# Smaller first and last chains on VectorE, a slightly changed preference on TensorE, and the last store on another queue, in an attention kernel

## Chip, cores, metric

One core of one Trainium2 chip. The metric is device time in microseconds (us); several executions of each kernel are timed, and kernels that are compared ran on the same chip in the same rounds. A few executions fell into a slow state (lower granted TensorE clock, 415 us and more); they are left out of the times and ratios below. All ratios compare with the kernel before in the same rounds.

## The reference

Grouped-query attention: 8 batches, 8 query heads, 2 key/value heads, 1024 positions, head size 64, float32.

```python
scores = scale * np.matmul(q_group, k_group.transpose(0, 1, 3, 2))
scores_max = np.max(scores, axis=-1, keepdims=True)
attn = np.exp(scores - scores_max)
attn = attn / (np.sum(attn, axis=-1, keepdims=True) + 1e-08)
output[:, q_start:q_end, :, :] = np.matmul(attn, v_group)
```

## The kernel before

The work is cut into 128 jobs (batch, head, half of the queries) of 8 cells (128 keys by 512 queries); a cell's exponentials are 65,536 numbers. ScalarE takes most cells, two at a time, with its exponential. VectorE takes some, with a bit trick: one instruction turns scores into the bits of a power of two (`p1`, L491), and then a **chain** of four steps corrects a group of cells at once: "and" (VectorE), "line" (GpSimd), "prod" and "add" (VectorE, two SBUF inputs each). TensorE computes the scores ("qk"), and, when a cell's exponentials are ready, the output ("pv"); VectorE normalises a finished job.

The order of all instructions is fixed beforehand by a planner, a small model inside the kernel. Each engine then works its list strictly in order, so one late step holds back everything behind it.

```python
GROUP, PARTS = 10, 2
CHAIN = ("and", "line", "prod", "add")
ON_POOL = ("line",)

def make_plan(nj, nkc):
    ...
    LIVE_A, LIVE_D, PENDING, PER_JOB, LEAD, RAMP, AHEAD, FIRST_PV = 28, 5, 16, 2, 6, 6, 0.0, 2.0
    AHEAD_D, EXTRA, LAST = 0, 0, 6
    ...
        if job_a < nj:                      # a score cell for ScalarE
            ...
                best = min(best or (INF,), (t - AHEAD, 1, "qk", 0, t))
        if job_d < nj and job_d <= job_a + lead + 1 and pending < PENDING:   # one for VectorE
            ...
        for i, (at, _, _, step) in enumerate(chainq):
            if CHAIN[step] in ON_POOL:
                at = max(at, pool, two_end)     # a line waits for VectorE's step to end
            else:
                at = max(at, dve, pool)         # and VectorE's step for the line
    ...
        elif kind == "p1":
            ...
            cur.append(cell)
            if len(cur) == GROUP:
                chainq.append((dve, d_id, cur, 0))
                cur = []
# ... (cut)
    def put_out(b, h, sides):
        rows = "(s p two) d -> p s two d"
        nc.sync.dma_start(
            out=out[b, h].rearrange(rows, p=128, two=2)[:, :, sides],
            in_=stage[(b, h)][:, :, sides],
        )
# ... (cut)
            if op[2] >= len(jobs) - 2:                       # the last two jobs: half stores
                at(op[0] + 0.01, put_out, b, h, slice(side, side + 1))
            elif ended.setdefault(op[2] // 2, op[2]) != op[2]:
                at(op[0] + 1.5, put_out, b, h, slice(0, 2))  # else one store for a pair
```

The softmax here doesn't subtract the row's maximum and nothing guards it: scores larger than these inputs give would overflow.

## Time and profile before

| | kernel before |
|---|---|
| time, median of 3 | 385.65 us (385.5 to 385.9) |
| span in the profile | 384.0 us |
| first activation starts / last one ends | 7.40 / 379.43 us |
| activations | 404 of two cells |
| cells on VectorE | 216 of 1024 |

The lines are in the prediction below. ScalarE runs one activation after another for 372 us; the time is their count, times their rhythm, plus what stands before the first and after the last.

### The profile page before, as it was taken

What the parts mean: (1) busy time and instruction counts of PE and PEld (TensorE: products, weight loads), DVE (VectorE), ACT (ScalarE), POOL (GpSimd) and SP (SyncE); (2) the same over time, 40 slices, a digit from 0 to 9 for tenths busy, and PEclk for the clock granted to TensorE, in tenths of its full rate; (3) what the DMA queues carried; (4) which work ended last, traced back from release to release, by engine and by line L of the source; (5) the groups of instructions that cost most, each with busy time, mean ns of one, the idle gap of its engine ahead of it and who ended that gap; (6) DMA issues with size and microseconds to landing.
All of it is one profiled execution on the core that took longest, in us unless ns stands there. A gap on an engine that the chain in (4) does not pass through costs nothing.

```text
span 384.0 us, 12026 instructions
## 1 busy us (share of the span) xinstructions
PE 365.6 (95%) x5172; PEld 233.6 (61%) x5172; DVE 353.8 (92%) x548; ACT 374.6 (98%) x409; POOL 174.4 (45%) x147
## 2 busy tenths in 40 slices
PE   8879898999999999999999999999999999998995
PEld 7425464666666666666666666666666666564664
DVE  4779998999999999999999999999999999989982
ACT  5999999999999999999999999999999999999995
POOL 5584535718244371563718245271643627040420
PEclk9999999999999999999999999999999999999999
DMA  8988988697756848585676759468675765711213
GB/s 137 135 152 135 130 154 124 129 147 140 113 109 132 140 103 139 101 156 103 139 131 120 130 106 152 96 126 137 105 124 123 138 102 119 126 56 29 57 56 84
DMA packets 102485, 45.48 MB, mean 118 GB/s; under 512 B 63792, under 2 KB 100976, under 8 KB 101184
## 3 DMA queue, kind: packets, MB, share of 16 engines
q1 hardware_dynamic: 82096, 31.21, 36.1%
q0 software_dynamic: 19712, 13.18, 32.3%
q8 instruction: 40, 0.66, 0.7%
q10 hardware_dynamic: 624, 0.33, 0.3%
q14 instruction: 13, 0.11, 0.1%
HBM read 25.17 MB, written 27.00 MB: 136 GB/s over the span
## 4 chain that ended last, share of the span: by engine, by line
ACT 86%; PE 10%; DVE 2%; issue 1%
ACT p_ring L477 86%; PE aps L466 4%; PE ops L538 4%; PE ops L409 1%; PE dps L466 1%; DVE pd L527 1%; DVE ost L554 0%; DVE y L525 0%; DVE z L512 0%; DVE rec L551 0%; PE dps L382 0%; PE dps L428 0%; PE ops L428 0%; PE aps L382 0%; DVE blank L288 0%
## 5 line engine op out<-in xcount | busy, mean ns | idle before, releaser
L477 ACT ACTIVATE p_ring<-aps 128x1024 bf16<-128x1024 f32 x404 | 371.8, 1067 | 1.4 <-PE aps L466 1.2
L466 PE MATMUL aps<-qT,kset 128*128 128x512 bf16 x808 | 239.9, 378 | 13.0 <-ACT p_ring L477 12.4
L538 PEld LDWEIGHTS <-p_ring 128*128 128x128 bf16 x3232 | 140.1, 98 | 64.0
L538 PE MATMUL ops<-vset,p_ring 128*128 128x65 bf16 x3232 | 154.6, 194 | 0.0
L491 DVE TENSOR_SCALAR pd<-dps 128x512 uint16<-128x512 f32 x216 | 138.6, 683 | 7.0 <-PE dps L466 6.7
L516 POOL TENSOR_SCALAR y<-z 128x5120 f16<-128x5120 uint16 (+1 forms) x22 | 96.4, 4383 | 70.0 <-DVE rec L551 48.7
L466 PEld LDWEIGHTS <-kset 128*128 128x128 bf16 x1024 | 79.7, 97 | 56.4 <-issue 25.8
L323 POOL DMA_DIRECT2D scr_q<-in_q_dram x63 | 39.1, 621 | 83.5 <-PE dps L466 44.3
L466 PE MATMUL dps<-qT,kset 128*128 128x512 bf16 x216 | 76.4, 379 | 0.0
L525 DVE TENSOR_TENSOR y<-z,y 128x5120 f16<-128x5120 uint16 (+1 forms) x22 | 61.0, 2772 | 1.1 <-POOL y L516 1.1
L527 DVE TENSOR_TENSOR pd<-pd,y 128x5120 uint16<-128x5120 uint16 (+1 forms) x22 | 60.9, 2769 | 0.1
L554 DVE TENSOR_TENSOR ost<-ops,rec 128x256 f32<-128x256 f32 x128 | 54.3, 425 | 4.4
L538 PEld LDWEIGHTS <-pd 128*128 128x128 bf16 x864 | 42.8, 98 | 24.7 <-DVE ost L554 2.2
L538 PE MATMUL ops<-vset,pd 128*128 128x65 bf16 x864 | 52.2, 194 | 0.3
L512 DVE TENSOR_SCALAR z<-pd 128x5120 uint16<-128x5120 uint16 (+1 forms) x22 | 32.3, 1467 | 0.5
L551 DVE RECIPROCAL rec<-ops 128x4 f32<-128x4 f32 x128 | 22.6, 176 | 9.6 <-PE ops L538 8.2
L323 POOL DMA_DIRECT2D scr_k<-in_k_dram x15 | 9.8, 656 | 39.9 <-PE aps L466 33.0
L356 POOL DMA_DIRECT2D vset<-in_v_dram x32 | 24.9, 784 | 0.0
L409 PE MATMUL ops<-blank 128*128 128x128 bf16 x40 | 5.3, 313 | 1.1 <-DVE blank L288 1.1
L409 PEld LDWEIGHTS <-blank 128*128 128x128 bf16 x40 | 4.4, 149 | 1.1 <-DVE blank L288 1.1
L363 POOL DMA_DIRECT2D kset<-kset x6 | 4.1, 684 | 0.0
L420 ACT ACT_TABLE_LOAD x1 | 1.3, 1283 | 1.8 <-issue 1.8
(23 smaller groups left out, 10.2 us busy)
## 6 DMA issues: line engine op xcount, KB each, us to landing
out_dram<-ost SPq DMA_DIRECT2D x63, 256.0 KB, 2.9
scr_q<-in_q_dram POOLq DMA_DIRECT2D x63, 128.0 KB, 3.5
kset<-kT SPq DMA_DIRECT2D x60, 64.0 KB, 3.1
vset<-in_v_dram POOLq DMA_DIRECT2D x32, 64.0 KB, 3.9
scr_k<-in_k_dram POOLq DMA_DIRECT2D x15, 128.0 KB, 3.7
qT<-scr_q SPq DMA_TRANSPOSE x63, 3.5
kset<-kset POOLq DMA_DIRECT2D x6, 128.0 KB, 4.3
fq<-in_q_dram ACTq DMA_DIRECT2D x2, 128.0 KB, 3.3
```

The costliest lines, as they stand in the source:

```text
L323: dma = nc.gpsimd.dma_start(out=scr.rearrange("(p f) -> p f", f=1024), in_=src.rearrange("(p s) d -> p (s d)", s=1024 // D),)
L356: nc.gpsimd.dma_start(out=vsets[b % 2][:, g, two * NHC : (two + 1) * NHC, 0:D], in_=v[b, g].rearrange("(c p two) d -> two p c d", p=128, t ...
L466: last_score[0] = nc.tensor.matmul(dst, lhsT=ksets[b % 2][:, h // HPG, side, c * 128 : (c + 1) * 128], rhs=qT[(b, h)], start=True, stop=Tr ...
L477: act = nc.scalar.activation(out=pt[:, 0:m], in_=psum.pop(("A", n))[:, 0:m], func=AF.Exp, scale=scale)
L491: nc.vector.tensor_scalar(out=groups[g][:, slot], in0=psum.pop(cell), scalar1=bits_scale, scalar2=bits_bias, op0=ALU.mult, op1=ALU.add,)
L512: eng.tensor_scalar(out=z, in0=pd, scalar1=0x7F, scalar2=None, op0=ALU.bitwise_and)
L516: eng.tensor_scalar(out=y, in0=z, scalar1=CURVE_A / 128.0, scalar2=CURVE_B, op0=ALU.mult, op1=ALU.add,)
L525: eng.tensor_tensor(out=y, in0=z, in1=y, op=ALU.mult)
L527: eng.tensor_tensor(out=pd, in0=pd, in1=y, op=ALU.add)
L538: nc.tensor.matmul(ops_of[s][:, qs, :], lhsT=p_of[cell][:, qs * 128 : (qs + 1) * 128], rhs=vsets[b % 2][:, h // HPG, c, :], start=opens an ...
L551: nc.vector.reciprocal(out=rec, in_=o[:, :, D])
L554: nc.vector.tensor_tensor(out=stage[(b, h)][:, :, side, :], in0=o[:, :, 0:D], in1=rec.unsqueeze(2).to_broadcast([128, NQS, D]), op=ALU.mult,)
```

## The change

The intent: let VectorE start on small chains so that its first results come early, end on small ones so that its last results are not late, and save the last store a place behind others on SyncE's queue. The diff, cut to its core (`per_job` with its zeros changes nothing):

```diff
-    ... AHEAD, FIRST_PV = 28, 5, 16, 2, 6, 6, 0.0, 2.0
+    ... AHEAD, FIRST_PV = 28, 5, 16, 2, 6, 6, 0.02, 2.0
+    FIRST_SIZES, FIRST_JOBS, FIRST_MORE = (3, 4, 6, 8), 0, 0
+    LAST_SIZE, LAST_GROUPS, LAST_JOBS, LAST_MORE = 4, 6, 6, 0
+    def size(g):
+        if g < len(FIRST_SIZES):
+            return FIRST_SIZES[g]
+        return LAST_SIZE if job_d >= nj - LAST_GROUPS else GROUP
-            if len(cur) == GROUP:
+            if len(cur) >= size(d_id):
-    def put_out(b, h, sides):
+    def put_out(b, h, sides, queue):
-        nc.sync.dma_start(
+        queue.dma_start(
-                at(op[0] + 0.01, put_out, b, h, slice(side, side + 1))
+                queue = nc.scalar if op[2] == len(jobs) - 1 else nc.sync
+                at(op[0] + 0.01, put_out, b, h, slice(side, side + 1), queue)
```

More of the change, by code (lines that the diff above doesn't have):

```diff
@@ L38, in make_plan @@
     FROM_PE, FROM_PV, FROM_ACT, FROM_DVE, FROM_POOL = 0.21, 0.16, 0.165, 0.10, 0.15
-    LIVE_A, LIVE_D, PENDING, PER_JOB, LEAD, RAMP, AHEAD, FIRST_PV = 28, 5, 16, 2, 6, 6, 0.0, 2.0
+    LIVE_A, LIVE_D, PENDING, PER_JOB, LEAD, RAMP, AHEAD, FIRST_PV = 28, 5, 16, 2, 6, 6, 0.02, 2.0
     INF = 1e9
-    AHEAD_D, EXTRA, LAST = 0, 0, 6
+    AHEAD_D = 0
+    FIRST_SIZES, FIRST_JOBS, FIRST_MORE = (3, 4, 6, 8), 0, 0
+    LAST_SIZE, LAST_GROUPS, LAST_JOBS, LAST_MORE = 4, 6, 6, 0
     FIRST_TURN, FIRST_LOAD, EACH_LOAD = 2.4, 4.5, 4.2
@@ L64, in first_free, with per_job @@
         return min(range(len(slots)), key=lambda s: slots[s])
+    def per_job(j):
+        if j < FIRST_JOBS:
+            return PER_JOB + FIRST_MORE
+        return PER_JOB + LAST_MORE * (j >= nj - LAST_JOBS)
+    def size(g):
+        if g < len(FIRST_SIZES):
+            return FIRST_SIZES[g]
+        return LAST_SIZE if job_d >= nj - LAST_GROUPS else GROUP
     while normed < nj:
@@ L73, in make_plan @@
         while job_d < nj and (
-            taken[job_d] >= PER_JOB + EXTRA * (job_d >= nj - LAST)
+            taken[job_d] >= per_job(job_d)
             or not todo[job_d]
@@ L576 @@
             if op[2] >= len(jobs) - 2:
-                at(op[0] + 0.01, put_out, b, h, slice(side, side + 1))
+                queue = nc.scalar if op[2] == len(jobs) - 1 else nc.sync
+                at(op[0] + 0.01, put_out, b, h, slice(side, side + 1), queue)
             elif ended.setdefault(op[2] // 2, op[2]) != op[2]:
-                at(op[0] + 1.5, put_out, b, h, slice(0, 2))
+                at(op[0] + 1.5, put_out, b, h, slice(0, 2), nc.sync)
         at(op[0], run[op[1]], *op[2:])
```

## The prediction

> **What bounds the kernel now.** I read the page's busy shares and its chain first, then the groups by line, then three short stretches of the timeline (start of the chain, about 30 us, about 368 us) and the end.
>
> ```profile
> PE 365.6 (95%) x5172; PEld 233.6 (61%) x5172; DVE 353.8 (92%) x548; ACT 374.6 (98%) x409; POOL 174.4 (45%) x147
> ...
> ACT 86%; PE 10%; DVE 2%; issue 1%
> ...
> L477 ACT ACTIVATE p_ring<-aps 128x1024 bf16<-128x1024 f32 x404 | 371.8, 1067 | 1.4 <-PE aps L466 1.2
> L466 PE MATMUL aps<-qT,kset 128*128 128x512 bf16 x808 | 239.9, 378 | 13.0 <-ACT p_ring L477 12.4
> ```
>
> ScalarE's exponentials (L477) are 371.8 of the 384.0 us span and had 1.4 us of visible idle, 1.2 of it before the first one. It is a single string: first start 7.40 us, last start 378.35 us, 403 spacings, so 370.95 / 403 = 0.9205 us each. The single start times in the trace have a smallest spacing of 0.903 and a median of 0.910. One activation lasts 1.067 us, longer than the spacing, so neighbours overlap by about 0.15 us and **short waits hide inside "busy"**: 0.9205 less some 0.912 of an undisturbed stretch is 0.0085 x 403 = 3.4 us. That is all the idle there is to win between first and last activation.
>
> Before the first activation and after the last nothing overlaps. The end, from the timeline:
>
> ```profile
> 378.35 1.08 ACT L477 ACTIVATE p_ring<-aps 128x1024 bf16<-128x1024 f32 x1
> ...
> 379.61 1.50 SPq L563 DMA_DIRECT2D out_dram<-ost  x3
> 379.95 0.18 DVE L551 RECIPROCAL rec<-ops 128x4 f32<-128x4 f32 x1 [0.37 <-PE ops L538]
> 380.17 0.42 DVE L554 TENSOR_TENSOR ost<-ops,rec 128x256 f32<-128x256 f32 x1
> ```
>
> Last activation ends 379.43; the last eight output matmuls (two cells) to 379.91; reciprocal and product to 380.59; the last store's issue starts 380.62; the wait on its landing ends 383.13; the closing barriers end at 384.03. That is 0.48 + 0.68 + 0.03 + 2.51 + 0.90 = 4.6 us of tail.
>
> Where did ScalarE lose its 3.4 us? Two places stand out in the spacings: 1.162 then 0.982 at 31.1 and 32.3 us (0.32 over 0.912), and 1.186 at 368.0 us (0.27). Both are TensorE standing in order behind VectorE:
>
> ```profile
> 27.13 2.83 DVE L527 TENSOR_TENSOR pd<-pd,y 128x5120 uint16<-128x5120 uint16 x1
> 30.01 0.54 PEld L538 LDWEIGHTS <-pd 128*128 128x128 bf16 x16 [0.35 <-DVE pd L527]
> 31.16 0.30 PEld L538 LDWEIGHTS <-pd 128*128 128x128 bf16 x8 [0.55 <-DVE ost L554]
> ```
>
> ```profile
> 363.80 2.81 DVE L527 TENSOR_TENSOR pd<-pd,y 128x5120 uint16<-128x5120 uint16 x1
> 366.53 0.95 DVE L512 TENSOR_SCALAR z<-pd 128x3072 uint16<-128x3072 uint16 x1
> 367.61 0.42 DVE L554 TENSOR_TENSOR ost<-ops,rec 128x256 f32<-128x256 f32 x1
> 368.08 0.30 PEld L538 LDWEIGHTS <-pd 128*128 128x128 bf16 x8 [0.64 <-DVE ost L554]
> ```
>
> Each time a ten-cell step of 2.8 us runs on VectorE, a normalisation (L551, L554) comes late behind it, the output accumulator is not free, and the score matmuls that ScalarE wants are queued behind. The long chains are what the change shortens. The rest of the 3.4 us is spread in crumbs of 0.03 to 0.08 us.
>
> **What the Trainium skill says.** "ScalarE: Activation LUTs", What ACT_TABLE_LOAD costs: an activation takes a fixed part plus 0.833 ns per element of the free dimension. Half of one (512 elements) is then 0.427 us. The trace of the kernel before has no half one and cannot confirm the slope; its 1.067 us for 1024 is near, not equal to, the page's 186 + 853 ns. "VectorE: DVE Perf Modes", The TRN2 errata: a small fixed cost per instruction, about 150 cycles measured (0.156 us at the page's 0.96 GHz). The trace agrees: from the 10- and 6-cell forms below the fixed parts come out at 0.15 to 0.17 us. "DMA: Bandwidth & Descriptors", Issuing engines are not separate DMA queues: several issuers save only the sequencer's time to issue. "DMA: Bandwidth & Descriptors", Anatomy of one DMA: a fixed cost of about 2 us, mostly the write's receipt; the section is on GpSimd's path, yet the last store here, from SyncE, shows 2.5 us.
>
> **The change part by part.**
>
> *ScalarE's share.* The order of instructions shows 404 activations of 128x1024 followed by one of 128x512, against 404: VectorE takes 215 cells instead of 216. The string gets one spacing more. The last start moves from 378.35 by 0.92 to 379.27, and its duration falls from 1.08 to about 1.08 - 0.43 = 0.65, so it ends at 379.92: **+0.49**. After it only one cell's four output matmuls are left instead of eight; at 0.03 us each: **-0.11**.
>
> *VectorE's chains.* 26 chains instead of 22, in sizes 3, 4, 6, 8, eighteen of 10, 4, 4, 4, 2. From these rows
>
> ```profile
> L525 DVE TENSOR_TENSOR y<-z,y 128x5120 f16<-128x5120 uint16 x21 | 59.2, 2820 | 1.1 <-POOL y L516 1.1
> L527 DVE TENSOR_TENSOR pd<-pd,y 128x5120 uint16<-128x5120 uint16 x21 | 59.2, 2817 | 0.1
> L512 DVE TENSOR_SCALAR z<-pd 128x5120 uint16<-128x5120 uint16 x21 | 31.3, 1491 | 0.5
> L525 DVE TENSOR_TENSOR y<-z,y 128x3072 f16<-128x3072 uint16 x1 | 1.8, 1759 | 0.0
> L527 DVE TENSOR_TENSOR pd<-pd,y 128x3072 uint16<-128x3072 uint16 x1 | 1.7, 1749 | 0.0
> L512 DVE TENSOR_SCALAR z<-pd 128x3072 uint16<-128x3072 uint16 x1 | 1.0, 954 | 0.0
> ```
>
> a cell costs (2.820-1.759)/4 = 0.265, 0.267 and 0.134 us, and an instruction a fixed 0.17, 0.15 and 0.15. Four chains more are 4 x 0.465 = +1.86; one cell less is 0.683 (L491) + 0.666 = -1.35. VectorE gains 0.5 us of work, to some 354.3: beside ScalarE's work, so **0** on the path in total. What counts is where: the first chain's results come after three cells, not ten, so output matmuls start earlier and the heap of them at 30 us shrinks; at the end the longest step is 4 cells, 0.15 + 4 x 0.267 = 1.2 us, not 2.8. That could remove all of 0.32 + 0.27 = 0.6. I do not take all: in the new order two chains stand interleaved at the start (4 and 6 cells) and at the end (4 and 4), with normalisations queued behind their steps and waits on GpSimd between, so smaller stalls may come back. I choose three quarters: **-0.45**.
>
> *The changed preference on TensorE (0.02 instead of 0).* ScalarE's score pair goes ahead of other work that is ready at nearly the same time. From the order of instructions I counted TensorE's work between two score pairs: slots that exceed the 0.912 us rhythm (two other scores and an output group, or one and three, and so on; a score is 0.2135 us, a group of four output matmuls 0.1225 by the timeline) are 65 before and 57 after. Priced by the mean excess that each kind shows now (0.030 for 2 and 1, 0.043 for 1 and 3, 0.074 for 2 and 2) that is 2.3 us against 2.25: nearly nothing. But the count cannot see which of them start late; the intent is to cut such crumbs. I choose **-0.4**, a weak number.
>
> *The last store over ScalarE's queue.* On SyncE the last issue began 0.03 us after the product ended; the store ahead of it (issue 380.03 to 380.53) was out in time. In the new order the last two normalisations stand further apart still. So the queue costs nothing now, and the landing is the same: **0** (+-0.1).
>
> Sum: +0.49 - 0.11 - 0.45 - 0.4 = -0.5, so 385.65 becomes about **385.15 us**; I say 385.1.
>
> **The rivals.** *A: only the extra half activation counts.* The stalls come back in other places, as the slot count hints: 385.65 + 0.49 - 0.11 = 386.0. For it speaks that 98% of the span is a string that got longer by half a link. *B: it all comes off.* Both big stalls vanish and half of the remaining 2.8 us of crumbs: 0.38 - 0.6 - 1.4 = -1.6, giving 384.0. For it speaks that the idle is real and small steps block less. *C: VectorE becomes the bound in an end stretch.* Six small chains alternate with GpSimd, where a four-cell line takes about 1.9 us, and VectorE is at 92% already; if one wait of 0.5 to 1 us reaches ScalarE beside A, 386.5 to 387. Against it: the last chain is two cells and its results are wanted only with the last activations. *D: the store's queue is the gain.* The timeline above gives it at most 0.1 us.
>
> **Range and chances.** My terms of doubt are about half a microsecond each for stalls and crumbs, and they are independent: the range is 384.2 to 386.1, between B and a little past A. Faster by over 2% would need less than 377.9; even with all 3.4 us won it would be 382.6. Slower by over 2% needs seven stalls of a microsecond. Chances: 0.01 faster, 0.98 within 2%, 0.01 slower.
>
> **What would show it.** In the profile after: 405 activations, the first at 7.4 us again, the last about 0.65 us long. The mean spacing should fall from 0.9205 to about 0.918; 0.9205 or more means A or C, 0.916 means B. Spacings over 1.1 us at about 31 and 368 us should be gone, and VectorE's busy time near 354.3. The tail from the last activation's end should be 4.4 to 4.6 us; less than 4.2 would mean that D was underrated. Wrong would be a time under 384.2 or over 386.1, and the mechanism would be wrong if the gain came from outside the string of activations.

## The result

384.73 us median (384.61 to 384.95, 6 runs) against 385.77 (385.36 to 385.93, 6 runs). The ratio is 0.9975, 95% interval 0.9962 to 0.9988. Ratios here are the mean time of one kernel's fast runs over that of the other's fast runs in the same rounds, so not quite the ratio of the medians quoted. The change is 1.0 us faster, a quarter of a per cent: within 2%, and inside the range.

The page of the changed kernel: busy times, chain, and ScalarE's group (count, then busy us and mean ns, then idle before).

```profile
PE 360.7 (94%) x5082; PEld 233.9 (61%) x5172; DVE 354.4 (92%) x559; ACT 374.5 (98%) x410; POOL 172.1 (45%) x151
...
ACT 96%; PE 1%; DMA 1%; issue 0%; DVE 0%
...
L490 ACT ACTIVATE p_ring<-aps 128x1024 bf16<-128x1024 f32 x405 | 371.8, 1085 | 1.3 <-PE aps L479 1.3
```

One activation more, the same busy time, and the chain that ended last is now ScalarE's at 96%; TensorE's share of it, 10% before, is 1%. (90 matmul records are missing in this trace, hence TensorE's lower sum.) The end, from the timeline:

```profile
378.29 0.37 SPq L576 DMA_DIRECT2D out_dram<-ost  x1
...
378.44 0.70 ACT L490 ACTIVATE p_ring<-aps 128x512 bf16<-128x512 f32 x1
...
379.53 0.18 DVE L564 RECIPROCAL rec<-ops 128x4 f32<-128x4 f32 x1 [1.27 <-PE ops L551]
379.75 0.42 DVE L567 TENSOR_TENSOR ost<-ops,rec 128x256 f32<-128x256 f32 x1
380.21 0.39 ACTq L576 DMA_DIRECT2D out_dram<-ost  x1
```

The last activation is a half one, and the last store is issued from ScalarE's queue; the store ahead of it was issued 1.92 us earlier, where in the kernel before it was 0.59 us.

Where the 0.92 us between the two profiles (spans of 384.03 and 383.12) came from, by the start times of single activations, counted from 0. "Excess" is a stretch's length over 0.912 us per activation:

| part | before | after | difference |
|---|---|---|---|
| activation 20 starts | 25.61 | 25.67 | +0.07 |
| excess, activations 20 to 40 | 0.51 | 0.13 | -0.38 |
| excess, 40 to 360 | 2.41 | 2.30 | -0.11 |
| excess, 360 to the last | 0.54 | 0.13 | -0.41 |
| one spacing more (0.91), a shorter last activation (1.085 to 0.70) | | | +0.53 |
| end of last activation to last product | 1.157 | 1.033 | -0.12 |
| the last store's landing | 2.53 | 2.03 | -0.50 |
| **sum** | | | **-0.92** |

Before activation 20 the changed kernel's profile starts 0.65 us earlier and then waits 0.7 us for a load (a spacing of 1.623 us that begins at 8.57 us). Other profiles show the same trade in other amounts, so it is not the change.

The tail gives 0.62 us of the gain, and most of that is the landing of one store, to which the prediction gave zero. The string of activations gives only 0.30 us net.

### The profile page after: what moved, and what is told of

Its sections match the earlier page's. It is cut to its first block, busy times and chain, and to the rows that moved or that the text cites. A ratio compares the mean times of both kernels' runs of the same rounds, so it can differ in the third digit from the quotient of the medians.

```text
span 383.1 us, 11952 instructions
## 1 busy us (share of the span) xinstructions
PE 360.7 (94%) x5082; PEld 233.9 (61%) x5172; DVE 354.4 (92%) x559; ACT 374.5 (98%) x410; POOL 172.1 (45%) x151
## 4 chain that ended last, share of the span: by engine, by line
ACT 96%; PE 1%; DMA 1%; issue 0%; DVE 0%
ACT p_ring L490 96%; PE ops L422 1%; DMA kset<-kset 1%; PE aps L479 0%; DVE ost L567 0%; PE dps L479 0%; PE ops L551 0%; PE dps L441 0%; PE dps L395 0%; DVE rec L564 0%; DVE blank L301 0%; ACT qT L451 0%; PE aps L395 0%; ACT kset L450 0%
## 5 line engine op out<-in xcount | busy, mean ns | idle before, releaser
L479 PE MATMUL aps<-qT,kset 128*128 128x512 bf16 x722 | 221.5, 378 | 11.6 <-ACT p_ring L490 10.5
L529 POOL TENSOR_SCALAR y<-z 128x5120 f16<-128x5120 uint16 (+5 forms) x26 | 97.1, 3736 | 72.9 <-DVE rec L564 36.4
L479 PE MATMUL dps<-qT,kset 128*128 128x512 bf16 x212 | 75.3, 378 | 2.1 <-DMA kset<-kset 0.7
L336 POOL DMA_DIRECT2D scr_q<-in_q_dram x63 | 36.7, 583 | 90.3 <-PE dps L479 44.6
L540 DVE TENSOR_TENSOR pd<-pd,y 128x5120 uint16<-128x5120 uint16 (+5 forms) x26 | 62.6, 2407 | 0.1
L538 DVE TENSOR_TENSOR y<-z,y 128x5120 f16<-128x5120 uint16 (+5 forms) x26 | 61.3, 2357 | 1.4 <-POOL y L529 1.4
L551 PEld LDWEIGHTS <-pd 128*128 128x128 bf16 x860 | 40.8, 97 | 25.5 <-DVE pd L540 2.8
L551 PE MATMUL ops<-vset,pd 128*128 128x65 bf16 x860 | 47.0, 194 | 1.2 <-DVE pd L540 0.3
L525 DVE TENSOR_SCALAR z<-pd 128x5120 uint16<-128x5120 uint16 (+5 forms) x26 | 32.8, 1267 | 0.4
L376 POOL DMA_DIRECT2D kset<-kset x6 | 3.1, 530 | 0.0
```

What stands on the lines that cost most here:

```text
L336: dma = nc.gpsimd.dma_start(out=scr.rearrange("(p f) -> p f", f=1024), in_=src.rearrange("(p s) d -> p (s d)", s=1024 // D),)
L479: last_score[0] = nc.tensor.matmul(dst, lhsT=ksets[b % 2][:, h // HPG, side, c * 128 : (c + 1) * 128], rhs=qT[(b, h)], start=True, stop=Tr ...
L525: eng.tensor_scalar(out=z, in0=pd, scalar1=0x7F, scalar2=None, op0=ALU.bitwise_and)
L529: eng.tensor_scalar(out=y, in0=z, scalar1=CURVE_A / 128.0, scalar2=CURVE_B, op0=ALU.mult, op1=ALU.add,)
L538: eng.tensor_tensor(out=y, in0=z, in1=y, op=ALU.mult)
L540: eng.tensor_tensor(out=pd, in0=pd, in1=y, op=ALU.add)
```

## The experiments

Each is named by its edit. Kernels are compared only within the same rounds. "Landing" is from the start of the last store's issue to the end of SyncE's wait on it.

### Was it the queue?

**Only the queue** (the kernel before with the last store on ScalarE's queue):

```diff
-                at(op[0] + 0.01, put_out, b, h, slice(side, side + 1))
+                queue = nc.scalar if op[2] == len(jobs) - 1 else nc.sync
+                at(op[0] + 0.01, put_out, b, h, slice(side, side + 1), queue)
```

> The kernel before, with only the last store moved to ScalarE's queue: 404 activations, chains of 10 as before. In the changed kernel the last store landed 2.0 us after its issue began, in the kernel before 2.5 us. If ScalarE's queue itself is quicker, the landing here is 2.0 us and the time about 385.3 (0.5 under the kernel before). If instead the landing is shorter because no other large store is in flight just ahead of it, this kernel still has the 256 KB store about 0.6 us ahead, the landing stays about 2.5 us and the time 385.75. The prediction said 0 +-0.1, that is, the second.

385.68 us (fast runs, 384.97 to 385.83), ratio 0.9996 (0.9983 to 1.0009): no gain. The profiled run was a slow one; its landing was 2.50 us.

**All but the queue** (the changed kernel with every store on SyncE):

```diff
-                queue = nc.scalar if op[2] == len(jobs) - 1 else nc.sync
+                queue = nc.sync
```

> The changed kernel, with the last store back on SyncE's queue; everything else as changed. If ScalarE's queue is quicker by itself: landing 2.5 us, time about 385.2. If the spacing of the stores did it: landing 2.0 us, time 384.75, no different from the changed kernel.

384.68 us, ratio 0.9976 (0.9964 to 0.9988), landing 2.01 us. From its timeline:

```profile
379.57 0.42 DVE L567 TENSOR_TENSOR ost<-ops,rec 128x256 f32<-128x256 f32 x1
380.02 0.37 SPq L576 DMA_DIRECT2D out_dram<-ost  x1
```

The issue follows the product at once, as on ScalarE. The queue is worth nothing; the landing is short on either.

### Was it the store ahead?

**Before, spread**: the kernel before, with the second last pair's 256 KB store issued at once and so ahead of, not between, the two half stores.

```diff
-                at(op[0] + 1.5, put_out, b, h, slice(0, 2))
+                late = 1.5 if op[2] < len(jobs) - 4 else 0.01
+                at(op[0] + late, put_out, b, h, slice(0, 2))
```

> The kernel before with one edit: the whole-pair store of the second last pair of jobs (256 KB) is issued as soon as its product is done, not 1.5 us later, so that it goes ahead of the last two half stores and not between them. The string of activations is untouched. If the last store lands late because a large store is in flight 0.6 us ahead of it: landing 2.0 to 2.2 us instead of 2.5, time about 385.3 (0.3 to 0.5 under the kernel before). If it lands late for another reason: 2.5 us and 385.75.

Fast runs 385.10 to 385.61 against 385.81 (385.71 to 386.35): ratio 0.9986 (0.9972 to 0.9999), some 0.5 us faster, with the string of activations untouched. That is the size of the landing's gain, though the interval only just leaves out no change. The profiled run was slow, as that of "only the queue": between these two slow ones, landing fell from 2.50 to 2.01 us.

**After, crowded**: the changed kernel, with the half store of job 126 held until the last reciprocal.

```diff
+        if behind:
+            tc.add_manual_dep(dma.ins, last_rec[0].name, SYNC, reason="crowd")
...
+                if op[2] == len(jobs) - 1:
+                    at(op[0] + 0.005, put_out, *held, nc.sync, True)
+                    at(op[0] + 0.01, put_out, b, h, slice(side, side + 1), queue)
+                else:
+                    held = (b, h, slice(side, side + 1))
```

> The changed kernel with one edit: the half store of the second last job (128 KB, SyncE's queue) is held back until the last job's reciprocal is done, so that it starts about 0.4 us ahead of the last store. If a store in flight just ahead delays the landing: landing 2.3 to 2.5 us instead of 2.0, time 385.0 to 385.2. If not: 384.73.

385.23 us (384.79 to 385.32), ratio 0.9978 (0.9965 to 0.9990), landing 2.15 us: a small part of the effect. A 128 KB store half a microsecond ahead costs little; the time does not resolve it. No run put a 256 KB store back there in the changed kernel.

All fast profiles together, the later experiments included:

| last store's queue | store just ahead | by how much (us) | landing (us) | in |
|---|---|---|---|---|
| SyncE | 256 KB | 0.59 | 2.53 | before |
| SyncE | 256 KB | 0.59 | 2.52 | only first |
| ScalarE | 256 KB | 0.57 | 2.54 | no small last |
| ScalarE | 256 KB | 0.69 | 2.43 | no small first |
| ScalarE | 128 KB | 0.47 | 2.15 | after, crowded |
| ScalarE | 256 KB | 1.28 | 2.04 | no preference |
| SyncE | 128 KB | 1.20 | 2.01 | only last |
| ScalarE | 128 KB | 1.29 | 2.03 | version B |
| SyncE | 128 KB | 1.41 | 2.01 | only the preference |
| SyncE | 128 KB | 1.91 | 2.01 | all but the queue |
| ScalarE | 128 KB | 1.92 | 2.03 | after |
| ScalarE | 128 KB | 2.38 | 2.04 | version A |

A 256 KB store within 0.7 us ahead costs 0.4 to 0.5 us, on either queue; at 1.28 us, in the one profile that has this, it costs nothing. In the changed kernel the planner's new order happens to put the pair's store ahead of job 126's, not between the last two.

### What each part of the chain sizes does

**No small first chains** (changed kernel, first chains of 10):

```diff
-    FIRST_SIZES, FIRST_JOBS, FIRST_MORE = (3, 4, 6, 8), 0, 0
+    FIRST_SIZES, FIRST_JOBS, FIRST_MORE = (), 0, 0
```

> The changed kernel with the first chains of 10 cells again (last chains of 4, preference 0.02 and ScalarE's queue kept). The order of instructions then has 407 full activations against 404 and a half: VectorE gets to 210 cells only. Theory 1 (the first small chains pay by letting VectorE take more cells early): 2.5 activations more at 0.92 us less at most 0.3 of crumbs, so about 386.7. Theory 2 (they pay by taking the stall near 30 us away): the stall of 0.3 comes back and the extra activations are hidden in former idle, about 385.1.

387.51 us (386.97 to 387.89), ratio 1.0047: slower than before. Theory 1 in direction, short in size by 0.8 us. There are 2.5 activations more; the stall is back as well (a spacing of 1.157 us from 30.6 us on), and the order of the last stores is the old one (landing 2.43). A further 0.3 us lies outside the span: these times are 2.1 us over the span in all six runs, those of the other kernels about 1.8.

**No small last chains** (changed kernel, last chains 10, 10, 4):

```diff
-    LAST_SIZE, LAST_GROUPS, LAST_JOBS, LAST_MORE = 4, 6, 6, 0
+    LAST_SIZE, LAST_GROUPS, LAST_JOBS, LAST_MORE = 10, 6, 6, 0
```

> The changed kernel with last chains of 10 cells again (the order shows last chains of 10, 10, 4; still 404 and a half activations). Theory 1 (small last chains pay in the string of activations, by removing the stall near 368 us): the spacings there show over 1.1 us again, time +0.3, about 385.0. Theory 2 (they pay in the tail, because the last chain's cells come ready earlier): the string is as in the changed kernel, and the time from the last activation's end to the last store's issue grows by 0.5 to 1.3 us, about 385.2 to 386. If neither holds: 384.7.

386.75 us (386.17 to 388.94), ratio 1.0035. Theory 2: from the 20th activation on the string is the changed kernel's, within 0.01 us in nearly every stretch, and the excess from activation 360 on is 0.13 in both. The tail is not: the last store's issue starts 2.33 us after the last activation ends, against 1.07, and a 256 KB store is right ahead.

```profile
380.57 0.92 SPq L576 DMA_DIRECT2D out_dram<-ost  x2
381.10 0.42 DVE L567 TENSOR_TENSOR ost<-ops,rec 128x256 f32<-128x256 f32 x1
381.56 0.39 ACTq L576 DMA_DIRECT2D out_dram<-ost  x1
```

+1.26 of issue and +0.5 of landing make 1.8 of the 2.0 us. The issue is late because TensorE still works through output matmuls for 1.61 us after the last activation (0.35 in the changed kernel). So the small last chains pay in the tail. The prediction's picture, long last chains bringing the stall near 368 us, does not hold: with chains of 10 at the end, that stall stays away, even though an add of 10 cells there takes 3.96 us instead of 2.82.

**Only small first chains** (kernel before plus the first sizes):

```diff
-    FIRST_SIZES, FIRST_JOBS, FIRST_MORE = (), 0, 0
+    FIRST_SIZES, FIRST_JOBS, FIRST_MORE = (3, 4, 6, 8), 0, 0
```

> The kernel before with first chains of 3, 4, 6 and 8 cells as its only change. The order of instructions has 406 full activations and a last chain of one cell. Theory 1 (the small first chains pay by themselves, the stall near 31 us goes): string +1.84 for two activations, less 0.4 for the stall; tail as before; about 387.1. Theory 2 (a last chain of one cell comes too late for the last activations, as with the preference at 0): over 387.5, with a spacing of 2 us or more, or a longer tail, in the last 15 us.

387.51 us (387.18 to 387.69), ratio 1.0046. The excess from activation 20 to 380 falls from 3.10 to 2.10 us, but there are two activations more, and the last product ends 1.84 us after the last activation, against 1.16. That is Theory 2's longer tail, but not for its reason: the one-cell chain is done at 377.10 us, 3.5 us before the last activation ends. TensorE has output matmuls left for 1.16 us after it, against 0.48.

**Only small last chains** (kernel before plus the last size):

```diff
-    LAST_SIZE, LAST_GROUPS, LAST_JOBS, LAST_MORE = 10, 6, 6, 0
+    LAST_SIZE, LAST_GROUPS, LAST_JOBS, LAST_MORE = 4, 6, 6, 0
```

> The kernel before with last chains of 4 cells as its only change: 404 and a half activations, as in the changed kernel; the stall near 31 us stays. If the small last chains bring the short tail by themselves (last store with no 256 KB store less than a microsecond ahead): landing 2.0 us, stall near 368 us gone: 385.7 + 0.5 - 0.4 - 0.5, about 385.3. If the order of the last stores stays as in the kernel before: landing 2.5 us and about 385.8.

387.63 us (386.59 to 388.35), ratio 1.0048: both expectations missed by two microseconds. The short landing came (2.01), but the string has a spacing of 3.3 us from 350.2 us on, and one of 1.7 right after it. The timeline there:

```profile
344.12 2.81 DVE L538 TENSOR_TENSOR y<-z,y 128x5120 f16<-128x5120 uint16 x1
344.28 4.83 POOL L529 TENSOR_SCALAR y<-z 128x2560 f16<-128x2560 uint16 x1 [0.77 <-DVE z L525]
...
346.96 4.82 DVE L540 TENSOR_TENSOR pd<-pd,y 128x5120 uint16<-128x5120 uint16 x1
...
351.84 0.65 PEld L551 LDWEIGHTS <-pd 128*128 128x128 bf16 x12 [2.15 <-DVE pd L540]
```

Two chains are interleaved. GpSimd's line on 5 cells takes 4.83 us instead of some 2.3 (0.19 + 5 x 0.427, from the 10- and 6-cell forms of the kernel before), and VectorE's add on 10 cells takes 4.82 instead of 2.82. Each seems to stand still while the other, which started first, runs. The product, first of the three, takes its usual 2.81 us and ends at 346.93. The line, begun at 344.28, ends 2.2 us after that, at 349.11. The add, begun at 346.96, ends 2.7 us after that, at 351.78. Those are about the 2.3 and 2.82 us that line and add take alone. TensorE waits 2.15 us for the add, and with it ScalarE. The Trainium skill, "SBUF — State Buffer", SBUF: two separate sides, describes this: the port pair that VectorE's instructions with two SBUF inputs share with GpSimd's reads is an exclusive lock, held for the whole instruction, and the later one "fully blocks". This trace agrees: had the two shared the ports, the product too would have been slowed. In the kernel before, no step of a chain is stretched by over 0.1 us.

### The preference

**No preference** (changed kernel, 0.0):

```diff
-    ... AHEAD, FIRST_PV = 28, 5, 16, 2, 6, 6, 0.02, 2.0
+    ... AHEAD, FIRST_PV = 28, 5, 16, 2, 6, 6, 0.0, 2.0
```

> The changed kernel with the preference for ScalarE's score pair back at 0. The order of instructions has 405 full activations and a half one, one more than the changed kernel. Theory 1 (the preference takes crumbs out of the string): one more activation, +0.92, and the sum of the spacings over 0.912 us after the twentieth activation rises from 2.6 to about 3.3 us, together 386.3. Theory 2 (only the count matters): 385.65, with the sum over 0.912 at 2.6 us.

387.89 us (386.96 to 388.04), ratio 1.0052; both theories missed. The excess from activation 20 to 380 is 2.15 us, less than the changed kernel's 2.52: here the preference takes no crumbs away. What it takes away is one activation and a collision:

```profile
369.81 1.22 DVE L538 TENSOR_TENSOR y<-z,y 128x2048 f16<-128x2048 uint16 x1
369.98 2.81 POOL L529 TENSOR_SCALAR y<-z 128x2048 f16<-128x2048 uint16 x1 [0.86 <-DVE z L525]
371.06 2.80 DVE L540 TENSOR_TENSOR pd<-pd,y 128x2048 uint16<-128x2048 uint16 x1
373.91 0.30 PEld L551 LDWEIGHTS <-pd 128*128 128x128 bf16 x8 [1.88 <-DVE pd L540]
...
374.81 1.02 ACT L490 ACTIVATE p_ring<-aps 128x1024 bf16<-128x1024 f32 x1 [1.58 <-PE ops L551]
```

The same sequence of three: a four-cell line of some 1.9 us takes 2.81 behind the product, and a four-cell add of 1.22 us takes 2.80 behind the line. TensorE waits 1.88, ScalarE 1.58 us of visible idle. The profiled run is the fastest of the four by 0.8 us, so the page explains less than the median.

**Only the preference** (kernel before, 0.02):

```diff
-    ... AHEAD, FIRST_PV = 28, 5, 16, 2, 6, 6, 0.0, 2.0
+    ... AHEAD, FIRST_PV = 28, 5, 16, 2, 6, 6, 0.02, 2.0
```

> The kernel before with the preference at 0.02 as its only change. The order of instructions has 407 full activations and a half one against 404: VectorE gets to 209 cells. Theory 1 (crumbs): string 3 spacings and a short one longer, +3.25, less some 1.5 of crumbs, about 387.5. Theory 2 (only the count): 389.0.

387.07 us (386.45 to 387.59), ratio 1.0029. Theory 1: the excess from activation 20 to 380 falls from 3.10 to 2.00 us. With chains of 10 the preference does take crumbs away, but VectorE then gets 209 cells and ScalarE four activations more (one a half).

The changed kernel itself has such a collision, at the start, where it harms nothing:

```profile
23.69 2.79 POOL L529 TENSOR_SCALAR y<-z 128x3072 f16<-128x3072 uint16 x1
...
24.99 2.56 DVE L540 TENSOR_TENSOR pd<-pd,y 128x2048 uint16<-128x2048 uint16 x1
```

The add of four cells, 1.21 us alone, takes 1.35 more, and yet the excess of activations 20 to 40 is only 0.13: ScalarE still has cells in hand there.

### Two versions meant to beat both

Both move the second last pair's store forward as in "before, spread", and need 403 activations (VectorE gets 218 cells).

Version A:

```diff
-    ... AHEAD, FIRST_PV = 28, 5, 16, 2, 6, 6, 0.02, 2.0
+    ... AHEAD, FIRST_PV = 28, 5, 16, 2, 6, 6, 0.03, 2.0
-    FIRST_SIZES, FIRST_JOBS, FIRST_MORE = (3, 4, 6, 8), 0, 0
-    LAST_SIZE, LAST_GROUPS, LAST_JOBS, LAST_MORE = 4, 6, 6, 0
+    FIRST_SIZES, FIRST_JOBS, FIRST_MORE = (3, 3, 5, 7), 0, 0
+    LAST_SIZE, LAST_GROUPS, LAST_JOBS, LAST_MORE = 3, 6, 6, 0
```

> A version meant to beat both: first chains 3, 3, 5 and 7, last ones of 3, preference 0.03, and the whole-pair store of the second last pair at once. The order of instructions has 403 full activations. If a fewer count and a short tail carry over: last activation ends 0.9 us earlier than in the changed kernel (one and a half spacings less, a full last one), about 383.8. If interleaved small chains meet GpSimd's line and are stretched in the last 20 us, a spacing of 1.5 us or more shows there and it is 385 or more.

384.02 us (383.18 to 384.24), ratio 0.9953 (0.9940 to 0.9966): the fastest here, 0.2% under the changed kernel by the ratios of each to the kernel before (the two were not run side by side, and their intervals touch). A spacing of 1.41 us from 26.5 us on follows a stretched product of VectorE (three cells in 1.59 us instead of an estimated 0.97), but the last 20 us are clear: no spacing there is over 1.07 us.

Version B:

```diff
-    FIRST_SIZES, FIRST_JOBS, FIRST_MORE = (3, 4, 6, 8), 0, 0
-    LAST_SIZE, LAST_GROUPS, LAST_JOBS, LAST_MORE = 4, 6, 6, 0
+    FIRST_SIZES, FIRST_JOBS, FIRST_MORE = (3, 4, 5, 6, 8), 0, 0
+    LAST_SIZE, LAST_GROUPS, LAST_JOBS, LAST_MORE = 4, 8, 6, 0
```

> As the version before, with first chains of 3, 4, 5, 6 and 8, last ones of 4 in the last eight jobs, preference 0.02: 403 full activations. Same two outcomes: about 383.8, or 385 and more with a stretched step of VectorE beside GpSimd's line in the last 20 us.

385.34 us, ratio 0.9991 (0.9977 to 1.0006): the gain of 403 activations is eaten by a spacing of 2.06 us from 373.6 us on and one of 1.48 from 27.4 us on.

```profile
370.73 2.38 POOL L529 TENSOR_SCALAR y<-z 128x1536 f16<-128x1536 uint16 x1 [1.15 <-DVE z L525]
371.81 2.37 DVE L540 TENSOR_TENSOR pd<-pd,y 128x2048 uint16<-128x2048 uint16 x1
374.23 0.30 PEld L551 LDWEIGHTS <-pd 128*128 128x128 bf16 x8 [1.16 <-DVE pd L540]
```

### The parts side by side

| kernel | activations | cells on VectorE | time (us) | ratio to before |
|---|---|---|---|---|
| before | 404 | 216 | 385.77 | 1 |
| only the queue | 404 | 216 | 385.68 | 0.9996 |
| only the preference | 407 and a half one | 209 | 387.07 | 1.0029 |
| only small first chains | 406 | 212 | 387.51 | 1.0046 |
| only small last chains | 404 and a half one | 215 | 387.63 | 1.0048 |
| no preference (both chain sizes) | 405 and a half one | 213 | 387.89 | 1.0052 |
| no small last (preference, first) | 404 and a half one | 215 | 386.75 | 1.0035 |
| no small first (preference, last) | 407 | 210 | 387.51 | 1.0047 |
| changed | 404 and a half one | 215 | 384.73 | 0.9975 |
| version A | 403 | 218 | 384.02 | 0.9953 |

No part gains by itself; three of four lose 1.3 to 1.9 us. No pair of the preference and the two chain sizes gains either: of their eight combinations, all run here, only the one with all three does. (Their last stores are on either queue, which is worth nothing.) It is the only one of the eight in which VectorE loses no more than one cell, no late spacing is long, and the last stores stand apart with few matmuls left before them.

## Why the prediction was right, and where it was not

The total (385.1 foretold, 384.73 measured) and the class were right; of the gain, -1.0 us measured, -0.5 was foretold. A string of activations that is a little longer but stalls less is what the profile shows: -0.36 foretold, -0.30 measured. But that is a third of the gain. The prediction said that its mechanism would be wrong if the gain came from outside the string, and 0.62 of 0.92 us came from the tail, where it foretold 0.11. For the larger part the mechanism was therefore missing. The terms, one by one:

- **The extra half activation**: +0.49 foretold, +0.53 measured; the half one took 0.70 us, not 0.65.
- **The tail's matmuls**: -0.11 foretold, -0.12 measured.
- **The two big stalls**: -0.45, three quarters of 0.6. Measured -0.38 in activations 20 to 40 and -0.41 from 360 on: all of it, and more. These stretches hold small waits too (one spacing of 1.07 us at 37.8 us in the kernel before), so the split between this term and the crumbs depends on where one cuts. I held back too much. But the reason given, the long last chains, is not it: without the small last chains the stall near 368 us stays away too. That the stall near 31 us belongs to the first chains is shown: the fast profiles of all four kernels with first chains of 10 have it (before, no small first chains, only the preference, only small last chains: spacings of 1.16 us that begin at 30.6 to 31.2 us), and none with first chains of 3, 4, 6 and 8.
- **The preference's crumbs**: -0.4, called weak. Measured -0.11 between activations 40 and 360. The slot count in the prediction, which gave nearly nothing, was the better guide. In the experiments the preference saves 1.1 us of excess with chains of 10 throughout, and none beside the small ones.
- **The last store**: this step failed in size. "The landing is the same: 0 (+-0.1)" was put down to the queue, and for the queue that is right. But the landing fell by 0.50 us because a 256 KB store was no longer 0.6 us ahead of it. I read from the timeline that the store ahead had been issued in time; I did not ask when it would have landed. The prediction's own test, a tail under 4.2 us (it was 3.98, against 4.60 before), told that a term was missing; the name that it gave, rival D, the queue, was the wrong one, since the queue gives nothing.
- **Rival C**, a wait of VectorE beside GpSimd, was dismissed for the changed kernel, rightly for its time. But in four of the other kernels it reached ScalarE, as an exclusive port, with single spacings 1.7 (no preference), 2.4 (only small last chains), 1.15 (version B) and 0.5 us (version A) over the rhythm.
- **The other signs**: VectorE's busy time was 354.4 us (354.3 foretold), and no spacing over 1.1 us is left at 31 or 368 us. The mean spacing was 0.920 us, not 0.918, because of the load waited for at 8.57 us; the profile of "all but the queue", with the same string and no such wait, has 0.918.

So two terms erred in opposite directions within the string (stalls 0.34 us more than foretold, crumbs 0.29 less); that they cancelled was luck. The missing 0.5 us of the landing is nearly the whole distance between forecast and measurement.

What stays open: why the preference and the chain sizes change how many cells VectorE gets was not tested, only counted in the order. Which part takes the stall near 368 us away is open too: from activation 360 on the excess is 0.13 to 0.20 us where the preference stands beside either chain size, and 0.42 to 3.46 with one part alone. And the runs of some slower kernels differ: "no preference" was profiled in its fastest run (386.96, the others 387.76 to 388.04), "only small last chains" in its slowest (388.35, the others from 386.59), and "no small last chains" ranges over 2.8 us. What differs between runs, a single profile each does not show.

## What to carry to other kernels

When engines work fixed lists in order, a planner's knobs have no value of their own: test the parts alone and together, and read for each the count of steps on the bounding engine, the stalls, and the tail. A transfer that nobody waits for can still lengthen the one that ends the kernel; keep large stores away from the last one (here 0.7 us was too near and 1.28 us enough). And chains interleaved between VectorE's two-input steps and GpSimd need room between them where the bounding engine has no work in hand.

## What the Trainium skill lacked or had wrong

- "DMA: Bandwidth & Descriptors", Anatomy of one DMA: the fit of 2.0 us plus bytes over 436 GB/s is for GpSimd's path and would give 2.3 us for 128 KB. A 128 KB store to HBM issued from SyncE or ScalarE landed in 2.01 to 2.04 us here with no store within 1.1 us ahead, and in 2.43 to 2.54 us with a 256 KB store 0.6 to 0.7 us ahead. No section gives the cost of a store in flight ahead.
- "ScalarE: Activation LUTs", What ACT_TABLE_LOAD costs: neighbouring activations are said to overlap by about 93 ns; here ones of 1.067 us on average follow at 0.910 us (median), an overlap of 0.16 us. That this hides idle of the bounding engine in its busy time is not said there.
- "SBUF — State Buffer", SBUF: two separate sides: the exclusive lock is described as measured here; what it lacks is a duration for this pair of operations. A four-cell add of 1.21 us took 2.36 to 2.80 us behind GpSimd's line, and a line of 5 cells 4.83 us behind VectorE's product instead of an estimated 2.3.
